# The head of a one-core hybrid decoder layer: order of the first loads, the transposes and the first two projection units

## Chip, cores and metric

The kernel runs on one core of a Trainium2 chip. The metric is the device time of one execution in microseconds (us), here the median of three runs. The engines are named as in the profile: PE (TensorE) does matmuls and transposes, PEld is its weight loads, DVE is VectorE, ACT is ScalarE, POOL is GpSimd and SP is SyncE, which issues the DMAs (SPq is its queue).

## What is computed

One post-norm layer over 256 tokens and 1024 channels, in float32. The input is normalized, projected to about 3,850 columns, these feed four mixers, and their outputs go through one output projection, a residual and a second normalization:

```python
h = _layernorm(x, emb_ln_g, emb_ln_b)
proj = jnp.einsum('bld,dn->bln', x, w_in)        # x is h here
(s_z, s_xbc, s_dt, h_q, h_f, h_i, h_g, r_q, r_k, r_v, r_g,
 m_q, m_k, m_v, m_g) = jnp.split(proj, idx, axis=-1)
y_ssd, y_hgrn = _ssd(...), _hgrn2(h_q, h_f, h_i, h_g, ...)
y_ret, y_moba = _retention(...), _moba(...)
y_cat = jnp.concatenate([y_ssd, y_hgrn, y_ret, y_moba], axis=-1)
y = jnp.einsum('blm,md->bld', y_cat, w_out)
return _layernorm(DEEPNORM_ALPHA * x + y, ln_g, ln_b)
```

## The kernel before

**Projection in units.** The columns of `w_in` are cut into units (`UNITS`): `h_f`, `h_q`, `h_i`, `m_q`, `m_k`, `xs`, `bc`, ... . A unit of 256 columns has two weight tiles of 512 KB: tile 0 holds rows of k tiles 0 to 3, tile 1 those of k tiles 4 to 7 (a k tile is 128 of the 1024 channels). Each raw tile (`wr_...`) is split into a rounded part `whi` (a cast, `split_hi`, on ACT unless said otherwise) and a rest `wlo` (a subtraction on DVE, `split_lo`). The normalized input, transposed, is split in the same way into `hhi` and `hlo`. A product is the sum of three matmuls: hi by hi (q = 0), whi with hlo (q = 1) and wlo with hhi (q = 2). A unit is 48 matmuls, for `h_f` and `h_q` of 256 columns each.

**Order.** The scheduler is off (`manual_schedule`): each engine runs its instructions in the order in which the Python code issues them and waits for semaphores where an operand is not there. There are 40 slots; `begin(slot)` issues the next weight load, the hi cast, the mixers' steps listed for that slot in `steps`, and the lo subtraction; `project(slot)` issues the matmuls. Raw weight tiles rotate through 5 buffers (`load_w`, line 204), so the sixth load, the second tile of `h_i`, waits until the first tile of `h_f` has been cast and subtracted. The loads after it wait in turn for the tiles that follow.

**The head.** Four 256 KB loads bring `x` (`xt`, line 161), then come the identity matrix (part of `ck`), the first unit's tiles in halves, `ch` (per-channel scales), and the rest. DVE takes statistics (line 266), POOL raises the variance to the power -0.5 (`lrs`, line 271), DVE and ACT normalize (`xn`, lines 276 and 279). PE transposes `xn` by k tile (`tr`, line 303), ACT scales each k tile out of PSUM (`hf`, line 314; for k = 0 directly `hhi`, line 311), DVE rounds it to `hhi` (line 318) and subtracts (`hlo`, line 324). In `first_unit` (lines 337 to 366) the transposes of k tiles 4 to 7 stand between the matmuls of `h_f` (line 346), then come `h_q` tile column 0 with q = 0 and 1, `h_f` with q = 2, `h_q` column 1, and at slots 2 and 3 `h_q` with q = 2.

**What follows.** At slot 0 `hgrn_gate` (line 474) takes the sigmoid of `h_f` on ACT, which gives `f`; `hgrn_key` gives `kk`; `hgrn_query` and `widen(1)` (lines 483 to 528) multiply `qk`, `A` and `kk` on DVE. `level(2)` and `level(4)` (line 545, tiles `lv`) are matmuls of `kk` and `A`; before `level(4)` DVE must have done `widen(2)` (lines 524 and 525).

Of the kernel before, what the change touches and what calls it, by code (L numbers as in the profile page):

```python
# [122 lines left out]
def hybrid_layer(  # L123
# [32 lines left out]


    xt = [sb([P, DM], f"xt{T}") for T in range(NT)]
    for T in range(NT):
        for hf in range(2):  # L160
            nc.sync.dma_start(xt[T][:, hf * 512:hf * 512 + 512],
                              x[T * P:(T + 1) * P, hf * 512:hf * 512 + 512])
    ch = cp.tile([P, C_FREE], F32, name="ch")
# [109 lines left out]
    def ln_apply(T, hf):  # L273
        cs = slice(hf * 512, hf * 512 + 512)
        if (T, hf) == (0, 1):
            nc.scalar.activation(xn[T][:, cs], xt[T][:, cs], AF.Identity, scale=lrs[T][:, 0:1],
                                 bias=lnb[:, 0:1])
            return
        nc.vector.tensor_scalar(xn[T][:, cs], xt[T][:, cs], lmv[T][:, 0:1], lrs[T][:, 0:1],
                                op0=ALU.subtract, op1=ALU.mult)  # L280
# [7 lines left out]
    nc.vector.scalar_tensor_tensor(lnb, lmv[0][:, 0:1], -1.0, lrs[0], op0=ALU.mult, op1=ALU.mult)
    split_hi(0, 0, 2, (0,))
    for hf in range(2):  # L290
        for T in range(NT):
            ln_apply(T, hf)
    split_hi(0, 0, 2, (1,))
    split_lo(0, 0, 2, (0,))
# [3 lines left out]
    trb = {}

    def h_transpose(k, T):  # L300
        if T == 0:
            trb[k] = bank(f"tr{k}")
        nc.tensor.transpose(trb[k][:, T * P:(T + 1) * P], xn[T][:, k * P:(k + 1) * P], ident)

    hfs = {}

    def h_in(k):
        hf = hfs[k] = sb([P, SEQ], f"hf{k}", tag="hf", bufs=4)
        g, b = ch[:, C_EG + k:C_EG + k + 1], ch[:, C_EB + k:C_EB + k + 1]
        if k == 0:  # L310
            nc.scalar.activation(hhi[:, k, :], trb[k][:, :SEQ], AF.Identity, scale=g, bias=b)
# [3 lines left out]
        if k == KT - 1:
            nc.scalar.copy(hhi[:, k, :], hf)
        else:
            nc.vector.tensor_copy(hhi[:, k, :], hf)
# [7 lines left out]
    for k in range(4):
        h_transpose(k, 0)
    for k in range(4):
        h_transpose(k, 1)
    for k in range(4):  # L330
# [6 lines left out]
    def first_unit():

        ps = [bank(f"pj_h_f{n}")[:, :SEQ] for n in range(2)]
        ps_of["h_f", 0], ps_of["h_f", 1] = ps  # L340

        def part(k, q):
            l = (whi, whi, wlo)[q][0, k // 4][:, k % 4]
            r = (hhi, hlo, hhi)[q]
            for n in range(2):
                nc.tensor.matmul(ps[n], l[:, n * P:(n + 1) * P], r[:, k, :], start=(k == 0 and q == 0),  # L346
                                 stop=(k == KT - 1 and q == 2))
        for k in range(KT):
            if k < 4:
                h_transpose(k + 4, 0)  # L350
                h_transpose(k + 4, 1)
                h_in(k + 4)
            if k == 1:
                split_hi(0, 1, 2, (1,), nc.vector.tensor_copy)
            part(k, 0)
            if k:
                part(k - 1, 1)
        part(KT - 1, 1)
        split_lo(0, 0, 2, (1,))
        split_lo(0, 1, 2)  # L360
        split_hi(1, 0)
        split_hi(1, 1)
        project(2, (0, 1))
        for k in range(KT):
            part(k, 2)
        project(3, (0, 1))

    def project(slot, parts=(0, 1, 2)):

        i, j = divmod(slot, 2)  # L370
        name = names[i]
        if name in PAIRS:
            p = slot - 2 * names.index(name)
            for T in range(NT):
                if p == 0:
                    ps_of[name, T] = bank(f"pj_{name}{T}")
                for k in range(2 * p, 2 * p + 2):
                    hi, lo = whi[i, j][:, k % 2, :], wlo[i, j][:, k % 2, :]
                    ts = slice(T * P, (T + 1) * P)
                    for q, (l, r) in enumerate(((hhi, hi), (hlo, hi), (hhi, lo))):  # L380
# [4 lines left out]
        def wk(k):
            hi = whi[i, k // 4][:, k % 4]
            return hi, wlo[i, k // 4][:, k % 4] if 2 in parts else hi
        if name in CHAN:
            if name == "h_q":
                if j not in hq:  # L390
                    hq[j] = bank(f"pj_h_q{j}")[:, :SEQ]
            elif j == 0:
# [742 lines left out]
```

## Time and profile before

| | |
|---|---|
| time, median of 3 runs | 150.19 us (150.09 to 150.38) |
| profiled execution, its own time | 150.68 us |
| its span | 149.0 us |
| PE busy | 137.5 us (92% of the span) |
| DVE / ACT / POOL busy | 116.5 / 75.0 / 17.8 us |
| mean granted TensorE clock | 0.971 |
| HBM read | 24.82 MB |

The span runs from the first to the last instruction of the execution; its own time is 1.68 us longer. Times in the rows are microseconds from the start of the span. Durations of instructions that follow each other on one engine overlap a little, so the distance from start to start is what a row of several costs.

### The profile page before, as it was taken

To read this page: it belongs to the slowest core of one execution; us is meant where nothing else is said; L and a number is where in the kernel's file an instruction comes from. 1 tells how busy PE (TensorE), PEld (TensorE's weight loads), DVE (VectorE), ACT (ScalarE), POOL (GpSimd) and SP (SyncE) were. 2 spreads that over 40 slices of the span, in tenths; PEclk is the share of its full clock that TensorE was granted. 3 is DMA by queue.
4 is the path that set the end of the run, shared out by engine and by line. 5 is a ranking of instruction groups with operands and counts; after the bars stand their busy time and mean duration, and the time that the engine had idled before them with its cause. 6 is when DMAs were issued, how large, how long until landed. Compare 5 with 4: busy or idle time off the path is not lost.

```text
span 149.0 us, 3073 instructions
## 1 busy us (share of the span) xinstructions
PE 137.5 (92%) x1224; PEld 122.5 (82%) x1224; DVE 116.5 (78%) x240; ACT 75.0 (50%) x122; POOL 17.8 (12%) x23
## 2 busy tenths in 40 slices
PE   5869999999999999999999999999999999999800
PEld 3149999999999998878899999999888888888800
DVE  1789968999596297969997599976989975478681
ACT  3088969742451759599709970054954635000000
POOL 4230000000000000000062018014004000004040
PEclk9996999999999999999999999999999999999975
DMA  4998399998748431595524830179774530000304
GB/s 141 328 384 312 95 292 342 324 319 317 201 139 258 136 60 80 148 272 165 163 101 145 306 119 4 35 232 383 243 239 141 159 127 0 0 0 0 141 0 141
DMA packets 9389, 26.05 MB, mean 175 GB/s; under 512 B 1056, under 2 KB 1696, under 8 KB 9120
## 3 DMA queue, kind: packets, MB, share of 16 engines
q1 hardware_dynamic: 9376, 25.87, 53.3%
q8 instruction: 9, 0.15, 0.4%
q14 instruction: 4, 0.03, 0.1%
HBM read 24.82 MB, written 1.05 MB: 174 GB/s over the span
## 4 chain that ended last, share of the span: by engine, by line
PE 81%; DVE 7%; DMA 3%; ACT 2%; SPq 1%; issue 1%; POOLq 1%; POOL 1%; DVEq 0%
PE pj_gg L381 8%; PE po L993 5%; PE po L994 5%; PE po L992 5%; PE pj_h_f L346 5%; PE pj_xs L420 4%; PE pj_m_k L420 4%; PE pj_m_g L420 4%; PE pj_r_k L420 4%; PE pj_m_q L420 4%; PE pj_h_i L420 4%; PE pj_zv L381 4%; PE pj_h_q L420 4%; PE pj_r_v L420 4%; PE pj_r_q L420 4%; DMA wr_h_f<-in_w_dram 3%
## 5 line engine op out<-in xcount | busy, mean ns | idle before, releaser
L992 PE MATMUL po<-whi_wo,yhi 128*128 128x512 f32 (+1 forms) x40 | 14.0, 350 | 0.0
L993 PE MATMUL po<-wlo_wo,yhi 128*128 128x512 f32 (+1 forms) x40 | 14.0, 349 | 0.0
L994 PE MATMUL po<-whi_wo,ylo 128*128 128x512 f32 (+1 forms) x40 | 13.9, 348 | 0.0
L234 DVE TENSOR_TENSOR wlo_wo<-wr_wo,whi_wo 128x1024 fp32r<-128x1024 f32 x8 | 9.6, 1219 | 0.0
L225 ACT CAST whi_wo<-wr_wo 128x1024 fp32r<-128x1024 f32 x8 | 8.2, 1050 | 2.3 <-PE pj_gg L381 1.7
L710 POOL TENSOR_SCALAR_AFFINE_SELECT ra<-ahi 128x1024 fp32r<-128x1024 f32 x1 | 1.1, 1101 | 65.0 <-DVE ahi L706 65.0
L992 PEld LDWEIGHTS po<-whi_wo,yhi 128*128 128x128 f32 x40 | 7.5, 188 | 1.1
L994 PEld LDWEIGHTS po<-whi_wo,ylo 128*128 128x128 f32 x40 | 7.5, 188 | 1.0
L993 PEld LDWEIGHTS po<-wlo_wo,yhi 128*128 128x128 f32 x40 | 7.5, 188 | 1.0
L225 ACT CAST whi_zv<-wr_zv 128x1024 fp32r<-128x1024 f32 x4 | 4.2, 1048 | 6.8 <-PE pj_xs L420 3.4
L179 PE MATMUL warm<-warm 128*128 128x512 f32 x6 | 5.5, 1088 | 1.5 <-DVE warm L176 1.5
L656 DVE SCALAR_TENSOR_TENSOR cacc_xs<-pj_xs,ch,cacc_xs 128x255 f32<-128x255 f32 (+2 forms) x6 | 2.9, 482 | 4.7 <-ACT cacc_xs L654 4.6
L381 PE MATMUL pj_zv<-whi_zv,hhi 128*128 128x512 f32 x16 | 6.5, 406 | 0.0
L381 PE MATMUL pj_gg<-whi_gg,hhi 128*128 128x512 f32 x16 | 6.4, 398 | 0.0
L1000 DVE TENSOR_TENSOR xn<-xn,po 128x512 f32<-128x512 f32 (+1 forms) x5 | 2.9, 580 | 4.4 <-PE po L994 4.4
L381 PE MATMUL pj_zv<-whi_zv,hlo 128*128 128x512 f32 x16 | 6.3, 394 | 0.0
L381 PE MATMUL pj_gg<-whi_gg,hlo 128*128 128x512 f32 x16 | 6.3, 394 | 0.0
L381 PE MATMUL pj_zv<-wlo_zv,hhi 128*128 128x512 f32 x16 | 6.3, 392 | 0.0
L381 PE MATMUL pj_gg<-wlo_gg,hhi 128*128 128x512 f32 x16 | 6.3, 392 | 0.0
L225 ACT CAST whi_gg<-wr_gg 128x1024 fp32r<-128x1024 f32 x4 | 4.2, 1046 | 2.5 <-DMA wr_gg<-in_w_dram 1.7
L793 ACT ACTIVATE ssq<-sy 128x512 f32<-128x512 f32 x1 | 0.6, 631 | 9.0 <-DVE sy L791 9.0
L860 ACT ACTIVATE pe<-pe,mmax 128x128 f32<-128x128 f32 (+1 forms) x8 | 3.5, 445 | 3.0 <-DVE mmax L853 3.0
(281 smaller groups left out, 494.1 us busy)
## 6 DMA issues: line engine op xcount, KB each, us to landing
wr_wo<-in_wo_dram SPq DMA_DIRECT2D x8, 512.0 KB, 3.9
wr_zv<-in_w_dram SPq DMA_DIRECT2D x4, 512.0 KB, 4.5
rb<-in_rows_dram SPq DMA_DIRECT2D x2, 1024.0 KB, 6.5
wr_gg<-in_w_dram SPq DMA_DIRECT2D x4, 512.0 KB, 4.9
wr_h_i<-in_w_dram SPq DMA_DIRECT2D x2, 520.0 KB, 5.3
xt<-in_x_dram SPq DMA_DIRECT2D x4, 256.0 KB, 3.7
wr_h_f<-in_w_dram SPq DMA_DIRECT2D x4, 256.0 KB, 5.0
wr_h_q<-in_w_dram SPq DMA_DIRECT2D x2, 512.0 KB, 6.7
```

Source lines behind the costliest of these rows:

```text
L179: nc.tensor.matmul(wb, warm[:, :P], warm, start=True, stop=True)
L225: copy(whi[i, j][:, r, :], t[:, r, :])
L234: nc.vector.tensor_sub(wlo[i, j][:, r, :], t[:, r, :], whi[i, j][:, r, :].bitcast(F32))
L346: nc.tensor.matmul(ps[n], l[:, n * P:(n + 1) * P], r[:, k, :], start=(k == 0 and q == 0), stop=(k == KT - 1 and q == 2))
L381: nc.tensor.matmul(ps_of[name, T], l[:, k, ts], r, start=(k == 0 and q == 0), stop=(k == KT - 1 and q == 2))
L420: nc.tensor.matmul(ps, l, r, start=(n == 0), stop=(n == len(seq) - 1))
L656: nc.vector.scalar_tensor_tensor(a_[:, d:], ps[:, :SEQ - d], tap(3 - d), a_[:, d:], op0=ALU.mult, op1=ALU.add)
L860: nc.scalar.activation(pt[:, h, :], pt[:, h, :], AF.Exp, bias=mmax[:, i:i + 1], accum_out=msum[:, i:i + 1])
L992: nc.tensor.matmul(po[T, c0], yhi[:, k, ts], hi, start=(i == 0 and j == 0), stop=False)
L993: nc.tensor.matmul(po[T, c0], yhi[:, k, ts], lo, start=False, stop=False)
L994: nc.tensor.matmul(po[T, c0], ylo[:, k, ts], hi, start=False, stop=(i == 3 and j == 1))
L1000: nc.vector.tensor_add(xn[T][:, cs], xn[T][:, cs], po[T, cs.start])
```

## The change

Seven edits, all in the head:

- `ch` is loaded by a DMA that ACT issues. SP's first loads stay the four of `x`; the identity's DMA goes, and the identity is made on POOL by a memset and an `affine_select`, ahead of POOL's memsets of `e1` and `yh`.
- `h_f` and `h_q` are loaded as four whole tiles, in a row, before the constants.
- The epsilon is added on DVE for both token tiles. `xn0` is normalized by ACT in two halves, `xn1` by DVE in four quarters.
- All 16 transposes stand ahead of the first matmul, token tile 0 first, in five PSUM banks.
- The halves of the casts of `h_f` and `h_q` stand between the k tiles (`CASTS`), on ACT and one on DVE.
- `h_f` and `h_q` are projected side by side by k tile with q = 0 and 1; then all four `wlo` and the 32 matmuls with q = 2.
- Both tiles of `h_i` are cast ahead of slot 0's sigmoids and subtracted behind them; `h_i` also takes its q = 2 matmuls last.

```diff
+    ch = cp.tile([P, C_FREE], F32, name="ch")
+    nc.scalar.dma_start(ch, chan)
     for T in range(NT):
...
-    nc.sync.dma_start(ck[:, :P], consts[:, :P])
...
+    nc.gpsimd.memset(ident, 1.0)
+    nc.gpsimd.affine_select(out=ident, in_=ident, pattern=[[1, P]], compare_op=ALU.is_equal, fill=0.0,
+                            base=0, channel_multiplier=-1)
...
-    load_w(0, 0, 2)
-    nc.sync.dma_start(ch, chan)
-    load_w(0, 1, 2)
+    for i in range(2):
+        for j in range(2):
+            load_w(i, j)
     nc.sync.dma_start(ck[:, P:], consts[:, P:])
-    for j in range(2):
-        load_w(1, j)
...
-        (nc.gpsimd, nc.vector)[T].tensor_scalar(lrs[T], lmv[T][:, 1:2], LN_EPS, None, op0=ALU.add)
+        nc.vector.tensor_scalar(lrs[T], lmv[T][:, 1:2], LN_EPS, None, op0=ALU.add)
...
+    for c in range(0, DM, 512):
+        nc.scalar.activation(xn[0][:, c:c + 512], xt[0][:, c:c + 512], AF.Identity,
+                             scale=lrs[0][:, 0:1], bias=lnb[:, 0:1])
+    for c in range(0, DM, 256):
+        nc.vector.tensor_scalar(xn[1][:, c:c + 256], xt[1][:, c:c + 256], lmv[1][:, 0:1],
+                                lrs[1][:, 0:1], op0=ALU.subtract, op1=ALU.mult)
+    split_hi(0, 0, 2)
...
+    for T in range(NT):
+        for k in range(KT):
+            nc.tensor.transpose(trb[k][:, T * P:(T + 1) * P], xn[T][:, k * P:(k + 1) * P],
+                                ident)
...
+    CASTS = {1: ((1, 0), (0,)), 4: ((0, 1), (0,)), 5: ((0, 1), (1,)), 6: ((1, 1), (0,)),
+             7: ((1, 1), (1,))}
...
+        nc.scalar.activation(hf, t, AF.Identity, scale=g, bias=b)
+        if k in CASTS:
+            split_hi(*CASTS[k][0], 2, CASTS[k][1])
+        nc.vector.tensor_copy(hhi[:, k, :], hf)
+        if k == 3:
+            split_hi(1, 0, 2, (1,), nc.vector.tensor_copy)
...
+        for k in range(KT + 2):
+            for i, d, q in ((0, 0, 0), (0, 1, 1), (1, 1, 0), (1, 2, 1)):
+                if 0 <= k - d < KT:
+                    part(i, k - d, q)
+        for i in range(2):
+            for j in range(2):
+                split_lo(i, j)
+            for k in range(KT):
+                part(i, k, 2)
...
-        if slot < 4:
+        if slot < 6:
             seq.sort(key=lambda kq: kq[1] == 2)
...
+        if slot == 0:
+            for j in range(2):
+                split_hi(2, j)
+            for j in range(2):
+                split_lo(2, j)
+        elif 1 < slot < 34:
             split_hi(*divmod(slot + 4, 2))
...
-        if slot > 1:
-            project(slot, (2,) if slot < 4 else (0, 1, 2))
+        if slot > 3:
+            project(slot)
```

On ACT, from the last k tiles to the sigmoids (`hf` are scaled k tiles, `sg` the sigmoids of `h_f`, `whi_...` casts of the unit named), there stood before:

```order
L314 ACTIVATE hf_245<-tr_242,ch 128x256
L314 ACTIVATE hf_256<-tr_253,ch 128x256
L316 CAST hhi<-hf_256 128x256
L225 CAST whi_h_q_287<-wr_h_q_98 128x1024
L225 CAST whi_h_q_289<-wr_h_q_100 128x1024
L225 CAST whi_h_i_349<-wr_h_i_106 128x1040
L474 ACT_TABLE_LOAD
L474 ACTIVATE sg_351<-pj_h_f_219 128x256
L475 ACTIVATE f<-sg_351,lbt 128x256
L474 ACTIVATE sg_354<-pj_h_f_220 128x256
L475 ACTIVATE f<-sg_354,lbt 128x256
```

and now:

```order
L230 CAST whi_h_q_193<-wr_h_q_100 128x512
L312 ACTIVATE hf_197<-tr_145,ch 128x256
L230 CAST whi_h_q_193<-wr_h_q_100 128x512
L230 CAST whi_h_i_364<-wr_h_i_107 128x1040
L230 CAST whi_h_i_366<-wr_h_i_109 128x1040
L455 ACT_TABLE_LOAD
L455 ACTIVATE sg_372<-pj_h_f_252 128x256
L456 ACTIVATE f<-sg_372,lbt 128x256
L455 ACTIVATE sg_375<-pj_h_f_253 128x256
L456 ACTIVATE f<-sg_375,lbt 128x256
L230 CAST whi_m_q_383<-wr_m_q_362 128x1024
L230 CAST whi_m_q_389<-wr_m_q_378 128x1024
```

The casts of `h_q` moved up between the k tiles, and the second cast of `h_i`, which stood behind the gates, stands ahead of the table load and the sigmoids.

On PE, where the matmuls of the first unit start (`tr` are transposes, `pj_h_f` and `pj_h_q` the sums of the two units, two of each), there stood before:

```order
L303 MATMUL tr4_221<-ck_76,xn0_110 128x128
L303 MATMUL tr4_221<-ck_76,xn1_111 128x128
L346 MATMUL pj_h_f0_219<-hhi_139,whi_h_f_0_130 128x256
L346 MATMUL pj_h_f1_220<-hhi_139,whi_h_f_0_130 128x256
L303 MATMUL tr5_230<-ck_76,xn0_110 128x128
L303 MATMUL tr5_230<-ck_76,xn1_111 128x128
L346 MATMUL pj_h_f0_219<-hhi_139,whi_h_f_0_130 128x256
L346 MATMUL pj_h_f1_220<-hhi_139,whi_h_f_0_130 128x256
L346 MATMUL pj_h_f0_219<-hlo_140,whi_h_f_0_130 128x256
L346 MATMUL pj_h_f1_220<-hlo_140,whi_h_f_0_130 128x256
```

and now:

```order
L341 MATMUL pj_h_f0_252<-hhi_139,whi_h_f_0_136 128x256
L341 MATMUL pj_h_f1_253<-hhi_139,whi_h_f_0_136 128x256
L341 MATMUL pj_h_f0_252<-hhi_139,whi_h_f_0_136 128x256
L341 MATMUL pj_h_f1_253<-hhi_139,whi_h_f_0_136 128x256
L341 MATMUL pj_h_f0_252<-hlo_140,whi_h_f_0_136 128x256
L341 MATMUL pj_h_f1_253<-hlo_140,whi_h_f_0_136 128x256
L341 MATMUL pj_h_q0_254<-hhi_139,whi_h_q_0_167 128x256
L341 MATMUL pj_h_q1_255<-hhi_139,whi_h_q_0_167 128x256
L341 MATMUL pj_h_f0_252<-hhi_139,whi_h_f_0_136 128x256
L341 MATMUL pj_h_f1_253<-hhi_139,whi_h_f_0_136 128x256
L341 MATMUL pj_h_f0_252<-hlo_140,whi_h_f_0_136 128x256
L341 MATMUL pj_h_f1_253<-hlo_140,whi_h_f_0_136 128x256
```

The transposes left the loop, and in their place come matmuls of `h_q` on the k tile before. On DVE the four `wlo` of `h_f` and `h_q` now all stand behind the last `hlo`, then both `wlo` of `h_i`, then `kk`; before, a quarter of them was done early and `kk` stood between the two of `h_i`.

## Rows read from the trace of the kernel before

**Rows 1.** Who waited for whom, engine PE, from 24 us to the end: waiter <- waited for: total us, times, longest us
```profile
PE lv L582 <- DVE F L528: 0.2, 1, 0.2
```

**Rows 2.** Stretches: us, busy (count) of PE PEld DVE ACT POOL, PEclk, DMA share, GB/s
```profile
7.00:10.50 3.50, 1.65 (x11) 1.19 (x12) 2.75 (x9) 2.48 (x5) 1.23 (x2) 1.00 1.05 373
10.50:13.75 3.25, 3.25 (x17) 3.22 (x17) 3.07 (x11) 3.07 (x7) 0.29 (x1) 0.50 1.01 381
...
14.00:24.00 10.00, 10.00 (x87) 10.00 (x86) 7.99 (x15) 8.67 (x12) 0.00 (x0) 1.00 0.69 219
```

**Rows 3.** Stretch of line 346 alone: PE and PEld busy (count), PEclk, DMA share, GB/s
```profile
10.25:13.95 3.70, 3.34 (x11) 2.62 (x12) 0.54 1.00 378
```

**Rows 4.** Timeline of PE: start us, us, engine line operation
```profile
24.03 0.28 PE L420 MATMUL pj_h_i<-whi_h_i,hhi 128*128 128x260 f32 x1
...
40.08 0.40 PE L545 MATMUL lv<-A,kk 64*64 64x64 f32 x12
```

**Rows 5.** Timeline, the normalization; [idle before <- released by] ends a row
```profile
4.78 1.51 DVE L266 BATCH_NORM_STATS2 lst<-xt 128x6 f32<-128x512 f32 x2 [0.57 <-DMA xt<-in_x_dram]
...
6.49 0.24 POOL L270 TENSOR_SCALAR lrs<-lmv 128x1 f32<-128x1 f32 x1 [4.25 <-DVE lmv L269]
6.81 0.57 POOL L271 TENSOR_TENSOR lrs<-lrs,mhalf 128x1 f32<-128x1 f32 x1
...
8.54 0.81 ACT L276 ACTIVATE xn<-xt,lnb,lrs 128x512 f32<-128x512 f32 x1
```

**Rows 6.** Tiles wr_h_f, wr_h_q, wr_h_i: issues (first to last), time to landing
```profile
L208 SPq DMA_DIRECT2D wr_h_f<-in_w_dram x4: 430/432/432, 3.1 to 5.0; - x4
...
DMA to landing us min/median/max: 4.9/5.0/5.1
...
L208 SPq DMA_DIRECT2D wr_h_q<-in_w_dram x2: 327/378/430, 6.4 to 6.8; - x2
...
DMA to landing us min/median/max: 6.2/6.7/7.2
...
L208 SPq DMA_DIRECT2D wr_h_i<-in_w_dram x2: 328/518/709, 9.1 to 16.3; - x2
...
DMA to landing us min/median/max: 3.4/5.3/7.2
```

**Rows 7.** Timeline of ACT, 10 to 25 us
```profile
10.23 1.46 ACT L314 ACTIVATE hf<-tr,ch 128x256 f32<-128x256 f32 x3
11.57 0.62 ACT L225 CAST whi_h_f<-wr_h_f 128x512 fp32r<-128x512 f32 x1
...
18.03 1.28 ACT L474 ACT_TABLE_LOAD   x1
20.34 0.39 ACT L474 ACTIVATE sg<-pj_h_f 128x256 f32<-128x256 f32 x1 [1.03 <-PE pj_h_f L346]
...
21.81 0.60 ACT L475 ACTIVATE f<-sg,lbt 128x256 f32<-128x256 f32 x1
...
23.27 2.10 ACT L225 CAST whi_m_q<-wr_m_q 128x1024 fp32r<-128x1024 f32 x2
```

**Rows 8.** Timeline of DVE, 14 to 41 us
```profile
14.31 1.30 DVE L324 TENSOR_TENSOR hlo<-hf,hhi 128x256 fp32r<-128x256 f32 x3
...
17.60 2.36 DVE L234 TENSOR_TENSOR wlo_h_q<-wr_h_q,whi_h_q 128x1024 fp32r<-128x1024 f32 x2
...
26.83 0.75 DVE L483 TENSOR_TENSOR qk<-pj_h_q,kk 128x256 f32<-128x256 f32 x2
...
33.79 0.69 DVE L509 TENSOR_TENSOR att<-ck,pc 128x512 f32<-128x512 f32 x1 [0.41 <-PE pc L500]
...
37.27 0.42 DVE L525 TENSOR_TENSOR kk<-kk,F 128x256 f32<-128x256 f32 x1
...
40.85 0.42 DVE L524 TENSOR_TENSOR A<-A,F 128x256 f32<-128x256 f32 x1 [1.82 <-PE lv L545]
```

More of the change, by code (lines that the diff above doesn't have):

```diff
@@ L158, in hybrid_layer @@
     xt = [sb([P, DM], f"xt{T}") for T in range(NT)]
+    ch = cp.tile([P, C_FREE], F32, name="ch")
+    nc.scalar.dma_start(ch, chan)
     for T in range(NT):
[L160 to L163, printed above, removed]
+        for c in range(0, DM, 512):
+            nc.sync.dma_start(xt[T][:, c:c + 512], x[T * P:(T + 1) * P, c:c + 512])
     ck = cp.tile([P, K_FREE], F32, name="ck")
-    nc.sync.dma_start(ck[:, :P], consts[:, :P])
     ident = ck[:, K_ID:K_ID + P]
@@ L172, in hybrid_layer @@
     nc.gpsimd.memset(mhalf, -0.5)
+    nc.gpsimd.memset(ident, 1.0)
+    nc.gpsimd.affine_select(out=ident, in_=ident, pattern=[[1, P]], compare_op=ALU.is_equal, fill=0.0,
+                            base=0, channel_multiplier=-1)
+    lnb = sb([P, 1], "lnb")
+    nc.scalar.copy(lnb, mhalf[:, 0:1])
     warm = sb([P, 512], "warm", tag="att")
@@ L259, in hybrid_layer @@
     lmv = [sb([P, 2], f"lmv{T}") for T in range(NT)]
-    lnb = sb([P, 1], "lnb")
     lrs = [sb([P, 1], f"lrs{T}") for T in range(NT)]
@@ L269, in ln_scale @@
         nc.vector.bn_aggr(lmv[T], lst[T])
-        (nc.gpsimd, nc.vector)[T].tensor_scalar(lrs[T], lmv[T][:, 1:2], LN_EPS, None, op0=ALU.add)
+        nc.vector.tensor_scalar(lrs[T], lmv[T][:, 1:2], LN_EPS, None, op0=ALU.add)
         nc.gpsimd.tensor_tensor(lrs[T], lrs[T], mhalf[:, :1], op=ALU.pow)
[L273 to L280, printed above, removed]
@@ L282, in hybrid_layer @@
     ln_stats(0, 0)
     ln_stats(0, 1)
+    ln_scale(0)
     ln_stats(1, 0)
-    ln_scale(0)
+    nc.vector.scalar_tensor_tensor(lnb, lmv[0][:, 0:1], -1.0, lrs[0], op0=ALU.mult, op1=ALU.mult)
     ln_stats(1, 1)
     ln_scale(1)
[L288 to L294, printed above, removed]
+    for c in range(0, DM, 512):
+        nc.scalar.activation(xn[0][:, c:c + 512], xt[0][:, c:c + 512], AF.Identity,
+                             scale=lrs[0][:, 0:1], bias=lnb[:, 0:1])
@@ L296, in hybrid_layer @@
+    for c in range(0, DM, 256):
+        nc.vector.tensor_scalar(xn[1][:, c:c + 256], xt[1][:, c:c + 256], lmv[1][:, 0:1],
+                                lrs[1][:, 0:1], op0=ALU.subtract, op1=ALU.mult)
+    split_hi(0, 0, 2)
     hhi = cp.tile([P, KT, SEQ], F32R, name="hhi")
     hlo = cp.tile([P, KT, SEQ], F32R, name="hlo")
[L298 to L303, printed above, removed]
+    trp = [bank(f"tr{j}").rearrange("p (k t) -> p k t", k=2) for j in range(5)]
@@ L305, in hybrid_layer @@
+    trb = [trp[(k + 1) // 2][:, (k + 1) % 2, :] for k in range(KT)]
+    for T in range(NT):
+        for k in range(KT):
+            nc.tensor.transpose(trb[k][:, T * P:(T + 1) * P], xn[T][:, k * P:(k + 1) * P],
+                                ident)
     hfs = {}
+    CASTS = {1: ((1, 0), (0,)), 4: ((0, 1), (0,)), 5: ((0, 1), (1,)), 6: ((1, 1), (0,)),
+             7: ((1, 1), (1,))}
     def h_in(k):
-        hf = hfs[k] = sb([P, SEQ], f"hf{k}", tag="hf", bufs=4)
+        hf = hfs[k] = sb([P, SEQ], f"hf{k}", tag="hf", bufs=6)
@@ L309, in h_in @@
         g, b = ch[:, C_EG + k:C_EG + k + 1], ch[:, C_EB + k:C_EB + k + 1]
+        t = trb[k]
         if k == 0:
-            nc.scalar.activation(hhi[:, k, :], trb[k][:, :SEQ], AF.Identity, scale=g, bias=b)
-            nc.vector.tensor_scalar(hf, trb[k][:, :SEQ], g, b, op0=ALU.mult, op1=ALU.add)
+            nc.scalar.activation(hhi[:, k, :], t, AF.Identity, scale=g, bias=b)
+            nc.vector.tensor_scalar(hf, t, g, b, op0=ALU.mult, op1=ALU.add)
             return
-        nc.scalar.activation(hf, trb[k][:, :SEQ], AF.Identity, scale=g, bias=b)
@@ L315, in h_in @@
[L315 to L318, printed above, removed]
+        nc.scalar.activation(hf, t, AF.Identity, scale=g, bias=b)
[4 more added lines that the diff above has]
+            split_hi(1, 0, 2, (1,), nc.vector.tensor_copy)
         h_rest(k - 1)
@@ L324, in h_rest, with first_units, part, project @@
         nc.vector.tensor_sub(hlo[:, k, :], hfs[k], hhi[:, k, :].bitcast(F32))
[L326 to L330, printed above, removed]
+    for k in range(KT):
         h_in(k)
-    split_hi(0, 1, 2, (0,))
     ps_of, hq = {}, {}
[L337 to L343, printed above, removed]
+    def first_units():
+        ps = [[bank(f"pj_{names[i]}{n}")[:, :SEQ] for n in range(2)] for i in range(2)]
+        for n in range(2):
+            ps_of["h_f", n], hq[n] = ps[0][n], ps[1][n]
+        def part(i, k, q):
+            l = (whi, whi, wlo)[q][i, k // 4][:, k % 4]
             r = (hhi, hlo, hhi)[q]
             for n in range(2):
[L346 to L368, printed above, removed]
+                nc.tensor.matmul(ps[i][n], l[:, n * P:(n + 1) * P], r[:, k, :],
+                                 start=(k == 0 and q == 0), stop=(k == KT - 1 and q == 2))
+        for k in range(KT + 2):
[5 more added lines that the diff above has]
+                split_lo(i, j)
+            for k in range(KT):
+                part(i, k, 2)
+    def project(slot):
         i, j = divmod(slot, 2)
@@ L386, in wk @@
             hi = whi[i, k // 4][:, k % 4]
-            return hi, wlo[i, k // 4][:, k % 4] if 2 in parts else hi
+            return hi, wlo[i, k // 4][:, k % 4]
         if name in CHAN:
[L389 to L392, printed above, removed]
+            if j == 0:
                 ps_of[name] = pp.tile([P, 2, SEQ], F32, tag="pp", name=f"pj_{name}")
-            ps = hq[j] if name == "h_q" else ps_of[name][:, j, :]
+            ps = ps_of[name][:, j, :]
             cs = slice(j * P, (j + 1) * P)
@@ L414, in project @@
         seq = [(k, q) for k in range(KT) for q in range(3)]
-        if slot < 4:
+        if slot < 6:
             seq.sort(key=lambda kq: kq[1] == 2)
         for n, (k, q) in enumerate(seq):
-            if q in parts:
-                l, r = trip(k)[q]
-                nc.tensor.matmul(ps, l, r, start=(n == 0), stop=(n == len(seq) - 1))
+            l, r = trip(k)[q]
+            nc.tensor.matmul(ps, l, r, start=(n == 0), stop=(n == len(seq) - 1))
     yhi = cp.tile([P, KT, SEQ], F32R, name="yhi")
@@ L1064, in begin @@
             load_w(*divmod(slot + 6, 2))
-        if slot < 34:
+        if slot == 0:
[4 more added lines that the diff above has]
+        elif 1 < slot < 34:
             split_hi(*divmod(slot + 4, 2))
@@ L1068, in begin @@
             st()
-        if slot < 34:
+        if 1 < slot < 34:
             split_lo(*divmod(slot + 4, 2))
-    first_unit()
+    first_units()
     lower_bound()
-    for q in (2, 3):
-        split_lo(*divmod(q, 2))
     for slot in range(s0):
         begin(slot)
-        if slot > 1:
-            project(slot, (2,) if slot < 4 else (0, 1, 2))
+        if slot > 3:
+            project(slot)
     order = [(i, T, n) for i, T in ((0, 0), (1, 0), (0, 1), (2, 0), (3, 0))
```

## Prediction

> **What bounds the kernel now.** I read the waits first, then the stretches with the granted clock, then the timelines of the head. From 24 us to the end PE waits once, for 0.2 us [rows 1]: behind the head the time is PE's own work, so the change is worth what it moves the start of that stretch, if nothing later gives it back. The stretches show how the head loses time [rows 2]: from 7.0 to 10.5 us PE is busy 1.65 of 3.50 us at a granted clock of 1.00 (2.4 GHz); from 10.5 to 13.75 it is busy all the time, at 0.50 (1.2 GHz); from 14 us on it is busy all the time at 1.00. The reader is to see that PE is not idle in the slow stretch but does half the work: up to 13.95 us it has taken up 12 of the 96 matmuls of `h_f` and `h_q` (12 weight loads [rows 3]), beside the last transposes. The other 84 end where `h_i` starts, at 24.03 us [rows 4]: 10.08 us, 0.12 us each.
>
> So two numbers decide: how many of the 96 are done when the clock is back, and whether a later operand is late. For the second, DVE's row at 40.85 us shows 1.82 us of idle time, and the one at 33.79 us 0.41 [rows 8]: at 40 us DVE is ahead of PE by some 2.4 us (`level(4)` starts at 40.08 [rows 4], its operand `kk` is done at 37.27 + 0.42 = 37.69). That is the cushion the change can use up.
>
> **Normalization.** Before, POOL adds the epsilon at 6.49 and takes the power at 6.81 for 0.57 us [rows 5]. The second statistic, bound by x's landing, runs from 4.78; of the row's 1.51 us for two the first ends near 5.5. Now aggregate and add follow at once: 0.5 us with hand-overs is an estimate (POOL's add, start to start, took 0.32). Power 6.0 to 6.6, bias 0.25, and ACT starts `xn0` at 6.85; two halves at 0.81, overlapping by 0.1, end at 8.4. That is about 1 us earlier than before, but I give it no credit by itself, because the next thing ACT needs is weights. The load of `ch` on ACT's queue runs beside x's first piece; it holds 19 KB, and costs 0 to 0.3 us (the upper end an estimate from the spread of 0.2 us in the landing times of equal `wr_h_f` pieces).
>
> **Weights.** All four tiles now stand in one line. Before, the second piece of `h_f` was issued near 3.55 and landed 5.0 us later, at 8.55 [rows 6]. The whole first tile now ends at that place in the line, less 64 KB of identity: 7.8 to 8.55. `h_q`'s first tile stands 1024 KB further on. Rates of landing before: from `h_q`'s first (6.4 + 6.2 = 12.6) to its second (6.8 + 7.2 = 14.0), 512 KB in 1.4 us, 366 KB/us; over the longer stretch from the first `h_f` piece (3.1 + 4.9 = 8.0) to 14.0, with small loads between, 1972 KB in 6.0 us, 329 KB/us. That gives 2.8 to 3.1 us and a landing between 10.6 and 11.65. I take 10.7, near the lower end, because the nearest row is the one for large pieces alone.
>
> **ACT's chain.** Start to start, an `hf` costs 0.46 us (three in 1.46, of which one lasts 0.56), a cast of half a tile 0.52 (0.62 less the overlap) [rows 7]. From 8.45: two casts, `hhi` of k = 0, `hf` of k = 1, and at 10.4 ACT wants `h_q`'s tile. It waits until 10.7. Then four half casts (2.08), five `hf` (2.30) and the last `hf` (0.57): `hf` of k = 7 is done at 15.65. In this chain a microsecond of late landing is a microsecond.
>
> **First gate, PE itself.** The first two matmuls run at 10.3, as before; the rest follow once DVE has rounded k = 1, at about 11.1, now with no transposes between. I assume the clock falls and rises where it did [rows 2]. Between 11.1 and 13.95, at twice 0.12 us or a little less (0.21 to 0.24), 12 to 13.5 fit: 14 to 15.5 done instead of 12. Three matmuls at 0.12 are 0.36 us. The rest is dense if operands keep up: PE reaches the q = 2 matmuls near 13.95 + 49 x 0.12 = 19.8, and the first `wlo` is done at 17.8 (below), the others every 1.14 us (2.36 us for two, the second lasting 1.22 [rows 8]) at 18.9, 20.1 and 21.2, where PE wants them at 20.8, 21.7 and 22.7. `h_i` starts 0.36 us earlier, at 23.67.
>
> **Second gate, the new chain through DVE and one load.** The buffer for `h_i`'s second tile comes free only when the first `wlo` is done, since all four subtractions now stand behind the last `hlo`. From `hf` of k = 7: the last cast to `hhi` and two `hlo` (1.30 for three [rows 8]) and a `wlo` of 1.22 make 2.15, so 17.8. Issue to landing took 3.4 us when that load was issued, at 16.3 [rows 6]: it lands at 21.3, 1.6 us later than before. And its cast now stands ahead of the sigmoids on ACT. Behind it come the table load and both sigmoids, and everything that DVE does with `f`. From landing: cast 1.05 (half of 2.10), table 1.31 with the gap, first sigmoid to last `f` 1.47 (20.34 to 21.81), then 0.5 and two casts of `m_q` 2.10, and a `wlo` of 1.2 [rows 7, 8]: `qk` starts 7.6 us after landing, at 28.9, 2.1 us later than before. From `qk` (26.83) to the end of `widen(2)` (37.69) DVE had 10.86 us, of which 0.41 idle [rows 8]: 10.45 of work in the same order. So `widen(2)` ends at 39.35. PE wants it at 40.08 - 0.36 = 39.72. It passes, with 0.4 us to spare; the cushion of 2.4 us is nearly gone. If `h_q` lands 0.4 us later, this gate decides, and from 0.7 us later on the kernel is slower.
>
> What lies behind `level(4)` keeps its distance: DVE had 1.82 us idle there [rows 8]. At nothing I cost the identity on POOL (x's landing hides it: the first transpose needs it at 7.7), the load of `ch` for its own use (needed at 9.5) and ACT's first table load behind it (done before 6.85); without the cover of x's landing the identity would cost what (d) says.
>
> **Sum.** 0.36 us off the profiled execution's 150.68 us gives 150.3; that execution lies 0.49 us above the median of 150.19, which I take as the base: 149.8.
>
> **Rivals.**
> (a) *The clock does not fall, or `h_q` lands early.* For it: `xn0` is ready 1 us sooner, so more transposes fall into 7 to 10.5 us. Against it: PE still waits for ACT between 10.4 and 11. PE then follows ACT; its last operand is rounded at 16.0, 16 matmuls and 32 more follow (5.8 us), and the second gate's 0.73 us is the limit: 149.45.
> (b) *`h_q` lands late.* At 11.65, by the lower rate, PE does about as much as before in the slow stretch, `widen(2)` ends at 40.3 and PE loses 0.2: 150.2 to 150.45. The gain is given back at `level(4)`.
> (c) *The clock stays low for a second stretch*, slower than before. PE's supply between 10.5 and 13.95 has holes that it had not (it was busy 3.25 of 3.25 us): waiting for `h_q` and for ACT's casts. If the clock is not raised near 13.9 but as late again, 3.4 us later, PE does 15 matmuls there instead of 29: 14 x 0.12 = 1.68 lost, less 0.36: 151.5. [...]
> (d) *POOL's code is loaded in front of the identity.* POOL now needs its code before the `affine_select`, ahead of two memsets and the powers. Before, it was loaded unseen in the 4.25 us that POOL sat idle ahead of 6.49 [rows 5], so the load lasts between 0 and 4.25 us. At the upper end the powers start near 7.0 instead of 6.0, `hf` of k = 7 comes 0.7 us later, and the second gate takes the gain: 150.2.
>
> Here the Trainium skill, "GPSIMD Engine Reference", section 2.1 on instruction dispatch, speaks against the change: the first call to a freshly loaded kernel pays about 6 us for its code, with no instruction in the profile. By its figure the powers would start near 8.7 and the time be about 151.8 (an estimate from the page). The trace does not agree here: code that is loaded behind the memsets was ready within the 4.25 us, so I hold to (d)'s bound.
>
> **Chances.** Forecast 0.42, (a) 0.13, (b) 0.21, (c) 0.16, (d) 0.08. A measurement of this kernel tells a change of 0.2% (0.3 us) from none. Of the forecast about nine tenths count as faster with all of (a), for 0.50; most of (b) and (d) and the rest of the forecast are no change, 0.26; (c) and the late end of (b) are slower, 0.24. The range reaches from (a) to short of (c)'s end: 149.2 to 151.1. The forecast alone would lie between 149.5 and 150.0.
>
> **What would show it.** Right: granted clock 0.50 for one stretch of about 3.4 us only; `h_i`'s first matmul near 23.7; ACT waiting for `wr_h_q` for 0.3 us near 10.4 and for the second `wr_h_i` near 20 to 21; `kk` of `widen(2)` done near 39.4 with PE not waiting. Wrong: a PE wait at `level(4)` (b), a clock of 0.50 past 14 us (c), the powers after 6.5 us (d), or a first matmul of `h_i` before 23.2 (a).

## Result and profile after

The changed kernel takes 151.26 us (median of 7 runs, 151.15 to 151.72), the kernel before 150.38 us beside it (7 runs, 149.79 to 150.89): 1.0063 of the time, 95% interval 1.0036 to 1.009. The forecast was 149.8, faster; the kernel became slower by 0.6%. The profiled execution took 151.67 us (span 149.9, mean granted clock 0.979), 0.99 more than that of before.

The waits of PE from 24 us to the end, as in [rows 1]:

```profile
PE lv L526 <- DVE kk L506: 0.9, 1, 0.9
PE lv L563 <- DVE F L509: 0.2, 1, 0.2
```

One wait is new: 0.9 us for `kk` at `level(4)`. The same stretches as in [rows 2]:

```profile
7.00:10.50 3.50, 1.40 (x9) 0.94 (x10) 1.61 (x5) 2.10 (x4) 0.55 (x1) 1.00 1.00 380
10.50:13.75 3.25, 3.25 (x16) 3.10 (x17) 2.55 (x9) 2.83 (x7) 0.00 (x0) 0.51 1.02 398
...
14.00:24.00 10.00, 10.00 (x87) 10.00 (x87) 9.29 (x18) 5.23 (x9) 0.08 (x1) 1.00 0.41 127
```

The clock falls to half and comes back as before (0.51 for 0.50, then 1.00), and PE is as full behind it. So the loss is not PE's rate. PE's timeline, for [rows 4]:

```profile
10.41 1.87 PE L297 MATMUL tr<-ck,xn 128*128 128x128 f32 x8 [1.69 <-DVE xn L286]
11.93 1.20 PE L341 MATMUL pj_h_f<-hhi,whi_h_f 128*128 128x256 f32 x4
...
24.15 0.28 PE L401 MATMUL pj_h_i<-whi_h_i,hhi 128*128 128x260 f32 x1
...
41.23 0.79 PE L526 MATMUL lv<-A,kk 64*64 64x64 f32 x32 [0.92 <-DVE kk L506]
```

`h_i` starts 0.12 us later than before (24.03) and `level(4)` 1.15 us later (40.08), of which 0.92 is the wait. The start of `level(4)` tells the time of all 14 executions that were profiled for this study: an execution's own time less that start lies between 110.32 and 110.76 us. What has to be explained is therefore why `kk` came late. ACT's timeline, for [rows 7]:

```profile
9.41 1.14 ACT L230 CAST whi_h_f<-wr_h_f 128x512 fp32r<-128x512 f32 x2 [1.40 <-DMA wr_h_f<-in_w_dram]
10.83 0.56 ACT L309 ACTIVATE hhi<-tr,ch 128x256 fp32r<-128x256 f32 x1 [0.28 <-PE tr L297]
11.29 0.56 ACT L312 ACTIVATE hf<-tr,ch 128x256 f32<-128x256 f32 x1
11.99 0.62 ACT L230 CAST whi_h_q<-wr_h_q 128x512 fp32r<-128x512 f32 x1
...
16.32 0.58 ACT L312 ACTIVATE hf<-tr,ch 128x256 f32<-128x256 f32 x1
...
23.14 1.06 ACT L230 CAST whi_h_i<-wr_h_i 128x1040 fp32r<-128x1040 f32 x1 [4.77 <-DMA wr_h_i<-in_w_dram]
24.22 1.28 ACT L455 ACT_TABLE_LOAD   x1
25.51 0.39 ACT L455 ACTIVATE sg<-pj_h_f 128x256 f32<-128x256 f32 x1
```

ACT stands idle for 4.77 us in front of the second cast of `h_i`, and the sigmoids, which stood at 20.34, wait behind it until 25.51. DVE, for [rows 8]:

```profile
17.82 2.35 DVE L239 TENSOR_TENSOR wlo_h_f<-wr_h_f,whi_h_f 128x1024 fp32r<-128x1024 f32 x2
...
27.61 0.43 DVE L460 TENSOR_SCALAR kk<-f 128x512 f32<-128x512 f32 x1 [2.14 <-ACT f L456]
...
30.83 0.74 DVE L464 TENSOR_TENSOR qk<-pj_h_q,kk 128x256 f32<-128x256 f32 x2
...
40.76 0.42 DVE L506 TENSOR_TENSOR kk<-kk,F 128x256 f32<-128x256 f32 x1
```

The first `wlo` ends at 17.82 + 1.22 = 19.04; only then is a raw buffer free and `h_i`'s second tile issued. Before, DVE did that subtraction in halves:

```profile
9.44 0.68 DVE L234 TENSOR_TENSOR wlo_h_f<-wr_h_f,whi_h_f 128x512 fp32r<-128x512 f32 x1
...
15.53 1.89 DVE L234 TENSOR_TENSOR wlo_h_f<-wr_h_f,whi_h_f 128x512 fp32r<-128x512 f32 x3
```

One half (an eighth of the four `wlo`, not a quarter) was done early; the other already stood behind the last `hlo` and ended near 16.2, and the load was issued at 16.3. So of the 2.8 us by which the load is issued later, 2.3 are the later end of the `hlo` (17.82 for 15.53, because ACT's last `hf` ends at 16.90 for 14.71), and 0.5 the half that is no longer done early.

The landing lines of `xt`, `wr_h_f`, `wr_h_q` and `wr_h_i` (issues first to last, then issue to landing), for [rows 6]:

```profile
L163 SPq DMA_DIRECT2D xt<-in_x_dram x4: 372/420/432, 0.8 to 2.1; - x4
...
DMA to landing us min/median/max: 2.7/3.4/6.0
...
L213 SPq DMA_DIRECT2D wr_h_f<-in_w_dram x2: 432/432/432, 2.6 to 3.1; - x2
...
DMA to landing us min/median/max: 6.8/7.2/7.6
...
L213 SPq DMA_DIRECT2D wr_h_q<-in_w_dram x2: 448/504/559, 3.6 to 4.1; - x2
...
DMA to landing us min/median/max: 8.4/8.8/9.2
...
L213 SPq DMA_DIRECT2D wr_h_i<-in_w_dram x2: 327/328/328, 8.1 to 19.1; - x2
...
DMA to landing us min/median/max: 4.0/5.9/7.9
```

First tiles land at 2.6 + 6.8 = 9.4 (`h_f`) and 3.6 + 8.4 = 12.0 (`h_q`), the second of `h_i` at 19.1 + 4.0 = 23.1. While that load waits for its buffer, the DMA engines do nothing (stretches of 1 us; the last two columns are DMA share and GB/s):

```profile
17.00:18.00 1.00, 1.00 (x11) 1.00 (x10) 1.00 (x4) 1.00 (x2) 0.00 (x0) 1.00 0.00 0
18.00:19.00 1.00, 1.00 (x11) 1.00 (x11) 1.00 (x2) 0.37 (x1) 0.00 (x0) 1.00 0.00 0
```

### The profile page after: what moved, and what is told of

It reads as the page before. It is cut to its first block, busy times and chain, and to the rows that moved or that the text cites. A ratio compares the mean times of both kernels' runs of the same rounds, so it can differ in the third digit from the quotient of the medians.

```text
span 149.9 us, 3068 instructions
## 1 busy us (share of the span) xinstructions
PE 137.6 (92%) x1224; PEld 122.4 (82%) x1224; DVE 116.8 (78%) x241; ACT 75.7 (50%) x125; POOL 17.7 (12%) x24
## 3 DMA queue, kind: packets, MB, share of 16 engines
HBM read 24.75 MB, written 1.05 MB: 172 GB/s over the span
## 4 chain that ended last, share of the span: by engine, by line
PE 61%; DVE 15%; DMA 8%; ACT 7%; issue 3%; SPq 2%; POOLq 1%; POOL 0%; DVEq 0%
PE pj_gg L366 8%; DMA wr_h_q<-in_w_dram 6%; PE po L974 5%; PE po L975 5%; PE po L973 5%; PE pj_r_k L401 4%; PE pj_xs L401 4%; PE pj_m_g L401 4%; PE pj_zv L366 4%; PE pj_r_v L401 4%; PE pj_r_q L401 4%; DMA wr_h_i<-in_w_dram 3%; PE pj_bc L401 2%; PE pj_m_k L401 2%; ACT hf L312 2%
## 5 line engine op out<-in xcount | busy, mean ns | idle before, releaser
L268 DVE BATCH_NORM_STATS2 lst<-xt 128x6 f32<-128x512 f32 x4 | 2.8, 692 | 4.0 <-DMA xt<-in_x_dram 4.0
L297 PEld LDWEIGHTS tr<-ck,xn 128*128 128x128 f32 x16 | 2.2, 168 | 4.3 <-ACT xn L283 2.2
```

## Experiments

Theory G: a chain sets the time, from `hf` of k = 7 through the first `wlo`, the freed buffer, `h_i`'s second tile, its cast ahead of the sigmoids, `kk`, `qk` and `widen(2)`. Rivals: PE's late start (the half-clock stretch, x late), and the order of the casts by itself. Ratios are to the kernel before, run beside each set on the same chip (150.24 to 150.48 us).

**A buffer more.**

```diff
+            if (i, j) == (1, 1):
+                t = sb(shape, f"wr_{name}_{j}", tag="xc")
...
```

> The changed kernel, with one edit: the second weight tile of h_q lies in a buffer that is free until later, so the second tile of h_i finds a free one and its load no longer waits for the first wlo. Theory G (the loss is the late load of h_i's second tile, issued at 19.1, landing at 23.1 us, behind which sigmoids, kk and widen(2) come): the load is issued near 9 us and lands before 18; the first sigmoid then waits only for PE's sums of h_f (about 22.3 instead of 25.5), widen(2) is done near 38.5 instead of 41.2, PE no longer waits 0.92 us at level(4), and the time falls from 151.26 by 0.9 to 150.35. Rival H (the loss is the late start of the matmuls, and the wait at level(4) only shows it): the time stays within 0.3 us of 151.26.

149.90 us (12 runs), 0.9978 (0.9957 to 0.9998). The load of `h_i` no longer waits for a `wlo`. Its timeline of PE:

```profile
24.39 0.28 PE L404 MATMUL pj_h_i<-whi_h_i,hhi 128*128 128x260 f32 x1
...
40.48 0.69 PE L529 MATMUL lv<-A,kk 64*64 64x64 f32 x32
```

`level(4)` waits for nothing and starts 0.75 us earlier than in the changed kernel, though `h_i` starts 0.24 us later. G holds, though the time fell further than its 150.35. The profiled execution is the slowest of the twelve: at 150.80 it lies 0.87 us below the changed kernel's profiled one, about the wait of 0.92, while the medians differ by 1.36 us. No trace shows the rest.

**The first `wlo` earlier, no buffer more.** The other end of the same chain: the first subtraction in halves behind k tiles 4 and 5.

```diff
         h_rest(k - 1)
+        if k in (4, 5):
+            split_lo(0, 0, 2, (k - 4,))
...
-                split_lo(i, j)
+                if i or j:
+                    split_lo(i, j)
```

> The changed kernel with one thing moved: the first subtraction wlo of h_f, in two halves, stands on DVE behind the rounding of k tiles 4 and 5 instead of behind the last hlo; no buffer more. Theory G: h_i's second tile is issued near 16.5 instead of 19.1 and lands near 20.5 to 21, 2 us earlier than in the changed kernel; widen(2) ends near 39.2 and PE does not wait at level(4), so the time falls to that of the run with the sixth buffer, 149.8 to 150.3. Rival (the sixth buffer won by letting the later loads run ahead, not by this one chain): the time stays at 150.8 to 151.3.

149.48 us (11 runs), 0.9939 (0.9916 to 0.9963): below both kernels, and lower than expected. Timelines of DVE, ACT and PE (the profiled execution, 150.29 us, is the slowest of the eleven):

```profile
15.68 0.68 DVE L239 TENSOR_TENSOR wlo_h_f<-wr_h_f,whi_h_f 128x512 fp32r<-128x512 f32 x1
...
19.95 1.07 ACT L230 CAST whi_h_i<-wr_h_i 128x1040 fp32r<-128x1040 f32 x1 [2.17 <-DMA wr_h_i<-in_w_dram]
...
37.59 0.43 DVE L509 TENSOR_TENSOR kk<-kk,F 128x256 f32<-128x256 f32 x1
...
39.53 0.69 PE L529 MATMUL lv<-A,kk 64*64 64x64 f32 x32
```

The subtraction ends 2.7 us earlier (16.36 for 19.04), the cast of `h_i` starts 3.2 us earlier, `kk` of `widen(2)` 3.2 us earlier, and PE finds it ready. It is the same work in another order: this chain was the loss.

**The gates first.** `h_i`'s second cast back behind the sigmoids, its `wlo` behind `kk`.

```diff
         if slot == 0:
-            for j in range(2):
-                split_hi(2, j)
-            for j in range(2):
-                split_lo(2, j)
+            split_hi(2, 0)
+            split_lo(2, 0)
...
+        if 0 == slot:
+            split_hi(2, 1)
+        if 1 == slot:
+            split_lo(2, 1)
```

> The changed kernel, with one edit: the second cast of h_i stands behind the sigmoids again, and its subtraction behind kk, as before the change; its load stays late. Theory G: the table load runs at 18.4, the sigmoids at 22.3 to 24.4, the cast at 24.4 to 25.4; widen(2) is done near 39.2, so PE does not wait at level(4), but the matmuls of h_i on k tile 4 wait about 0.3 us for the cast: 150.6 (150.4 to 150.9). If the place of the cast did not matter and only the load's landing did, the time would stay at 151.26.

150.56 us (12 runs), 1.0021 (1.0000 to 1.0041), as expected. PE's waits from 24 us on:

```profile
PE pj_h_i L401 <- ACT whi_h_i L230: 0.3, 1, 0.3
PE lv L563 <- DVE F L509: 0.2, 1, 0.2
```

The wait at `level(4)` is gone, and a smaller one stands in its place: the late cast of `h_i` now stops PE directly.

**The cast order alone, in the kernel before.**

```diff
-        if slot < 34:
+        if slot == 0:
+            for j in range(2):
+                split_hi(2, j)
+        elif 1 < slot < 34:
             split_hi(*divmod(slot + 4, 2))
```

> The kernel before with one edit of the change alone: the second cast of h_i moved ahead of the table load and the sigmoids. Theory G (the cast order costs only together with the late load that all subtractions behind the last hlo bring): here the load is issued at 16.3 as before and lands at 19.7, so the cast ends near 20.8, the first sigmoid starts near 22.1 instead of 20.34 and qk near 28.6 instead of 26.83; the cushion of 2.4 us at level(4) shrinks to about 0.6 and the time stays within 0.2% of before (150.0 to 150.6 against 150.3). Rival (the order alone costs it): slower by 0.5 us or more, with a PE wait at level(4).

150.97 us (12 runs), 1.0027 (1.0007 to 1.0047): both expectations missed. It is slower, but not at `level(4)`. PE's waits from 7 us on:

```profile
PE tr L303 <- DVE xn L279: 2.3, 2, 2.1
PE pj_h_i L420 <- DVE wlo_h_i L234: 0.7, 1, 0.7
PE lv L582 <- DVE F L528: 0.2, 1, 0.2
```

In the kernel before the second `wlo` of `h_i` stands behind `kk`, so late gates make `h_i` itself late: it began at 23.33, 0.7 us earlier than before, and lost that again in the wait. The change had moved that `wlo` ahead of `kk`, and there the price shows at `level(4)`. So the cast order costs something without the late load too.

**`ch` later, or the weights in halves.** Two tries at the landings, `nc.sync.dma_start(ch, chan)` behind `h_f`'s first tile, and `load_w(i, j, 2)` for the four tiles.

> The changed kernel, with one edit: ch is issued by SP behind h_f's first tile instead of by ACT ahead of x. In the changed kernel x's last piece landed 6.0 us after its issue (8.15 us; 6.4 before), h_f's first tile at 9.4, h_q's first at 12.0. Theory C (the second queue, ACT's, with 128 small packets beside x, holds x back): x's last piece lands near 6.4 again, h_f's first tile near 8.6, h_q's near 11, hf of k = 7 is done 1 us earlier (15.9 instead of 16.9), widen(2) near 40.2, and the time falls by 0.6 to 1.0, to about 150.4. Rival D (whole tiles of 4 KB a partition right behind x hold it back): the landings and the time do not change by more than 0.3 us.

> The changed kernel, with one edit: the four tiles of h_f and h_q are loaded in two halves each, as before the change those of h_f were (packets of 2 KB instead of 4 KB, eight DMAs instead of four). Rival D (large packets right behind x hold its last piece back): x's last piece lands near 6.4, h_f's first half near 8.0, and the time falls by 0.6 to 1.0, to about 150.4. Theory C (ACT's queue does): x's last piece still lands near 8.1 and the time stays within 0.3 us of 151.26, or rises a little since SP issues four more DMAs at 0.45 us each ahead of h_i's first tile.

151.72 us (6 runs), 1.0096 (1.0062 to 1.013), and 151.96 us (6 runs), 1.0101 (1.0068 to 1.0134). Neither queue nor size of packets cured the time. On the landings both expectations missed: x's last piece came 5.0 and 4.9 us after its issue, between the 4.2 of before and the 6.0 of the changed kernel, and then `h_i`'s second load took 4.7 us in both instead of 4.0. The profiled execution with `ch` later tells more than its time, by stretch and by timeline of PE:

```profile
10.50:13.75 3.25, 2.84 (x17) 2.17 (x17) 2.27 (x8) 2.72 (x7) 0.29 (x1) 1.00 1.04 403
...
23.32 0.28 PE L402 MATMUL pj_h_i<-whi_h_i,hhi 128*128 128x260 f32 x1
...
41.25 0.79 PE L527 MATMUL lv<-A,kk 64*64 64x64 f32 x32 [1.07 <-DVE kk L507]
```

The clock is full here, and PE reaches `h_i` 0.83 us sooner than in the changed kernel; `level(4)` starts at 41.25, for 41.23 there. With the halves `h_i` starts at 22.66, 1.49 us sooner, and PE waits 1.07 us at `level(4)` too. PE's late start is refuted as the cause: a head start of PE is waited away.

**Everything later.** One more 256 KB load of x between x and the weights (`nc.sync.dma_start(dose, x[0:P, 0:512])`).

> The changed kernel with one more load of 256 KB (the first half of x's first token tile once more, into a buffer that nothing reads) between x and the weights. At 366 KB/us the four weight tiles land 0.7 us later. Theory G (a chain from the landings through ACT, the first subtraction, the freed buffer, h_i's second tile, its cast, the sigmoids and widen(2) sets the time): the time grows by 0.5 to 0.8 us over the changed kernel's 151.26, to 151.8 to 152.1, and the PE wait at level(4) is about 1.6 us. Rival (PE's own dense work sets the time): under 0.3 us, 151.5 or less.

151.77 us (6 runs), 1.0102 (1.0061 to 1.0143): 0.5 us more than the changed kernel, just under G's window and outside the rival's. In its profiled execution PE waits 1.0 us at `level(4)` and 0.3 at `pj_m_q`, less than the 1.6 expected; x landed early there. The intervals of this run and of the changed kernel overlap, and the two runs on the landings, with no load more, took as long (151.72 and 151.96), so this run decides nothing.

**Filling PE's idle time.** One matmul of 128 x 512 that nothing reads, between the transposes of the two token tiles: in the changed kernel, with the sixth buffer, and with the early `wlo`.

```diff
+        if T == 0:
+            nc.tensor.matmul(wb, warm[:, :P], warm, start=True, stop=True)
```

> The changed kernel with only the extra matmul between the transposes, the buffers as in the change. Theory G: the clock stays up and PE reaches h_i 0.5 to 0.9 us earlier, but level(4) then waits 1.5 to 1.8 us instead of 0.9 and the time stays 151.1 to 151.5. Rival (the half-clock stretch is what makes the changed kernel slower): 150.4 or less.

> The changed kernel with h_q's second raw tile in a buffer of its own (as in the sixth-buffer run) and one more matmul of 128 x 512 that nothing reads, between the transposes of the two token tiles, where PE stood idle for 1.5 us. Theory G with the chain out of the way: PE's own work is the bound again, so the clock of the head is worth something: no stretch at 0.5 or 0.6, h_i starts near 23.3 to 23.7 instead of 24.4, all executions at a mean clock of 0.982 or more and near 149.7 (the sixth-buffer run had ten executions at 149.65 to 150.05 with clocks of 0.982 to 0.992 and two at 150.75 to 150.8 with 0.970 to 0.973). Rival: where x lands early the extra matmul delays the second half of the transposes by up to 1.4 us, and the time is 150.2 or more.

> The same with the extra matmul between the transposes. Theory G: with level(4) out of the way PE's own head decides, so the time is 0.3 to 0.6 us below the run without the extra matmul, 149.2 to 149.8, as the sixth buffer with the extra matmul showed (149.33). Rival (in this order the rounding of k tiles 6 and 7, now 0.6 us later, holds PE up): no difference to the run without it.

And in the kernel before, between the transposes of its first four k tiles, alone and with the sixth buffer:

> The kernel before with the extra matmul of 128 x 512 that nothing reads, between the transposes of the first and the second token tile of k tiles 0 to 3. Theory P (before, PE's own work from 10.5 us on sets the time, and its half-clock stretch costs what the clock takes there): the clock stays at 1.00 from 7 to 24, the second transposes come 0.4 to 0.7 us later, the 12 matmuls that PE had done by 13.95 become about 18, and the time falls by 0.3 to 0.8 us to 149.7 to 150.2 (before 150.48). Then most of what the fill-and-buffer version won is the clock's and not the reordering's. Rival (the fill delays ACT's chain by as much as it gives): 150.3 to 150.9.

> The kernel before with the extra matmul and with h_q's second raw tile in a buffer of its own. Both theories: the buffer adds nothing here, because DVE had 2.4 us to spare at level(4), so the time is within 0.2 us of the run with the extra matmul alone. If the reordering itself is worth something, this stays 0.3 us or more above the 149.33 of the changed kernel with the same two edits.

| | as it is | with the extra matmul |
|---|---|---|
| before | 150.24 to 150.48 | 150.39, 1.0019 (0.9987 to 1.0052) |
| before, sixth buffer | not run | 150.40, 1.0024 (0.9992 to 1.0056) |
| changed | 151.26, 1.0063 | 151.06, 1.0016 (0.9986 to 1.0045) |
| changed, sixth buffer | 149.90, 0.9978 | 149.33, 0.9928 (0.9903 to 0.9952) |
| changed, early `wlo` | 149.48, 0.9939 | 149.38, 0.9942 (0.9912 to 0.9971) |

In the changed kernel alone the clock of the profiled execution is 1.00 from 10.5 to 13.75 us, `h_i` starts only 0.26 us earlier (23.89), and the wait takes it back. Of PE's waits from 7 us on:

```profile
PE lv L528 <- DVE kk L508: 1.0, 1, 1.0
```

That wait was to be 1.5 to 1.8 us. This execution, 151.72 us, is also the slowest of the twelve: four took 150.07 to 150.41, and no trace shows what they gained.

With the sixth buffer the extra matmul is worth 0.57 us between the medians (the intervals just do not touch), and 149.33 is below the 149.7 expected. With the early `wlo` it is worth nothing that the runs can tell: the time lies in my window, but the gain of 0.3 to 0.6 us did not come. The rival had said so, yet its mechanism is not seen: in both versions PE waits only once for a rounded k tile, for 0.3 us. The stretches with the sixth buffer and the extra matmul:

```profile
7.00:10.50 3.50, 2.86 (x18) 2.04 (x18) 2.03 (x7) 2.81 (x6) 0.55 (x1) 1.00 1.00 395
10.50:13.75 3.25, 2.97 (x21) 2.51 (x20) 2.85 (x10) 3.25 (x9) 0.48 (x1) 1.00 1.01 325
```

In the kernel before it wins nothing that shows in time, though its clock is at 1.00 in the profiled execution too and `level(4)` starts 0.42 us earlier, at 39.66; my window of 149.7 to 150.2 was missed. With both the buffer and the matmul the order of before takes 150.40 us and the changed order 149.33: 1.1 us by the medians, 1.4 by the ratios. The early `wlo`, with neither, is 0.9 us below the kernel before by its ratio. So the reordering is worth about 1 us once its load is freed. Why the early `wlo` does as well without the extra matmul stays open; in its profiled execution the clock was 1.00 from 7 to 13.75 us without it.

## Why the prediction was wrong

**The step that failed is the landing terms of the second gate.** The prediction let `h_q`'s first tile land at 10.7, within 10.6 to 11.65; it landed at 12.0, outside the bounds. The rate was not the error: 1024 KB from 9.4 to 12.0 are 394 KB/us, faster than the 329 to 366 used. The base was: `h_f`'s first tile came at 9.4, not between 7.8 and 8.55, because x's last piece landed late (its statistic started at 8.15, before at 6.43). And the 3.4 us for the last load was 4.0. Together 1.3 and 0.6 us, against a spare of 0.4. The last statistic of x on DVE, before:

```profile
6.43 0.69 DVE L266 BATCH_NORM_STATS2 lst<-xt 128x6 f32<-128x512 f32 x1
```

and after:

```profile
8.15 0.69 DVE L268 BATCH_NORM_STATS2 lst<-xt 128x6 f32<-128x512 f32 x1 [1.70 <-DMA xt<-in_x_dram]
```

The late x held up this chain on a second path that the prediction left out: the second half of the transposes waited for it until 10.41, so ACT got to `hhi` of k = 0 at 10.83 and was ready for the `h_q` cast only near 11.75. That is 1.05 of the 1.3 us even if `h_q` had landed at 10.7. The split between the two landings is not fixed either: in the execution with `ch` later the `h_q` cast began at 11.30 and the last load took 4.7 us, 0.6 and 1.3 us too much, and `level(4)` started at the same time. Also, 10.7 lay at the low end of the prediction's own range: its middle, 11.1, uses up the spare.

**Link by link the chain was right.** From the `h_q` cast to the end of the last `hf`: 4.95 us forecast, 16.32 + 0.58 - 11.99 = 4.91 measured. From there to the end of the first `wlo`: 2.15 and 2.14. From landing (the start of the waiting cast) to `qk`: 7.6 and 30.83 - 23.14 = 7.7. From `qk` to the end of `widen(2)`: 10.45 and 10.35. `widen(2)` ended at 41.18 instead of 39.35, which is 1.83 us late, nearly the sum of the two landing errors, and the warning "from 0.7 us later on the kernel is slower" came true.

**First gate.** 14 to 15.5 matmuls were forecast by 13.95; line 341 shows ten weight loads there (the stretch of [rows 3]):

```profile
10.25:13.95 3.70, 2.02 (x9) 2.09 (x10) 0.54 0.99 387
```

The second half of the transposes waited 1.69 us for `xn1` and then ran in the half-clock stretch, so `h_i` began at 24.15, not 23.67. This cost nothing: `level(4)` waited anyway.

**Normalization** was right for the first token tile (power at 5.69, forecast 6.0; `xn0` at 6.49, forecast 6.85) and silent on the second, whose x piece was late.

**Rivals.** (b) came, at its place and by a late `h_q`, but late through x and not through the lower rate that (b) named, and with 0.9 us where its bound allowed 0.2: the bound was two rates from one execution, and held no spread of the landings themselves. (a) did not: the clock fell. (c) did not: 1.00 from 14 us on. (d) did not. POOL's timeline:

```profile
0.82 0.20 POOL L172 MEMSET ck<- 128x128 f32 x1
1.10 0.29 POOL L173 TENSOR_SCALAR_AFFINE_SELECT ck<-ck 128x128 f32<-128x128 f32 x1
...
5.69 0.57 POOL L273 TENSOR_TENSOR lrs<-lrs,mhalf 128x1 f32<-128x1 f32 x1 [2.94 <-DVE lrs L272]
```

The `affine_select` starts 0.28 us behind the memset's start, and the power as soon as its operand is there. The 6 us that the Trainium skill, "GPSIMD Engine Reference", section 2.1, gives for the first call to a freshly loaded kernel do not show here.

## What to carry to other kernels

When a cast in an engine's fixed order waits for a load, ask what frees that load's buffer and when: whatever makes the freeing work later (here a longer chain in front of it, and half of it no longer done early) makes the load later by as much, and the load's whole issue-to-landing time stands on the path. The cure is to move that work up or to give the load a buffer. A spare of 0.4 us on a chain with two landings in it is no spare, since the landings alone moved by more than 1 us between executions; such a chain needs its bound from several executions, or a low chance.

## What the runs showed of the hardware that was not expected

- With the same first loads x's last 256 KB landed 4.2 to 6.0 us after issue in seven profiled executions, `h_f`'s first tile at 7.8 to 9.4 and `h_q`'s at 10.6 to 12.0. In the four executions with the loads of before it landed 4.2 to 4.4 us after issue, and the last statistic of x started at 6.43 to 6.58. Whether the whole weight tiles right behind x cause it was not settled: halves brought 4.9 us.
- The 520 KB load of `h_i`, alone when issued (the next load followed 1.1 to 1.2 us later, with the early `wlo` 2.5), took 3.4 to 3.6 us in the five executions that issued it at 16.1 to 16.4, and 4.0 to 4.8 in the six that issued it at 17.8 to 19.1. This took part of every head start; its cause is open.
- The mean granted clock from 10.5 to 13.75 us was 0.51 in the changed kernel and 0.63 with the sixth buffer (1.2 GHz for most of it), and 1.00 (2.4 GHz) with the gates first and with the early `wlo`, though PE's instructions in the head are the same in all four. In the 3.5 us ahead of it PE had been busy 1.40, 1.53, 2.72 and 2.26 us, and x's last statistic had started at 8.15, 8.02, 6.83 and 7.28.
